# Three edits to a hybrid decoder layer: attention's last score columns, the third channel tile's outputs, and three weight sums

## The chip, the cores and the metric

The kernel runs on one core of one Trainium2 chip. The metric is the device time of one execution, in microseconds (us). Before the change it was 1298.82, 1296.9 and 1293.77 us in three runs, 1296.9 in the median. PE is the matrix engine (TensorE), DVE VectorE, ACT ScalarE, POOL GpSimd, SP SyncE, which issues most of the DMAs.

## What is computed

One decoder layer on 16 meta tokens and 1024 tokens of width 1024, all in float32:

```python
h = jnp.concatenate([meta, x], axis=1)
a = rmsnorm(h, ln_mix_pre[l])
proj = a @ w_in[l]
dq, dk, dv, hq, hf, hi, hg = jnp.split(proj, SPLITS, axis=-1)
y_diff = diff_attention(dq, dk, dv, ...)      # 4 heads, causal, two softmaxes: p[0] - lam * p[1]
y_hgrn = hgrn2(hq, hf, hi, hg, ...)           # 4 heads, a gated recurrence in chunks of 16
mix = jnp.concatenate([y_diff, y_hgrn], axis=-1) @ w_out[l]
h = h + rmsnorm(mix, ln_mix_post[l])
a = rmsnorm(h, ln_ffn_pre[l])
y = conv_ffn(a, w_ffn_up[l], ffn_conv_w[l], ffn_conv_b[l], w_ffn_down[l])
h = h + rmsnorm(y, ln_ffn_post[l])
...
# conv_ffn: u = a @ w_up (5632 channels), a causal convolution of width 3 over the
# sequence for each channel, then gelu(gate) * up, then @ w_down
```

## The kernel before

**Precision.** Every float32 product is made of three matmuls on a high and a low part of each operand (hi x hi, hi x lo, lo x hi). Making the parts is work of ACT (the cast `uh`), and of DVE or POOL (the rest `ul`).

**Order of the work.** The order of PE's rows is written out by the program: generators of attention, recurrence and projections are taken in turn by `interleave`, so that projections fill PE while attention waits. The order on DVE, ACT, POOL and SP is made by the scheduler of the tile layer; `tc.issue_after(x)` pins what is issued within it behind the instruction x. Operations of DVE, ACT and POOL go through one helper and all carry line L58.

**Attention** runs for each of four heads over nine blocks of rows, of which the last, block 8, sees 1040 columns. `scores` (L653 to L707) makes the scores of a block for two maps m, with the projection's rows between them. PSUM is a pool of eight banks (L972): two buffers of one bank under the name `ip`, two of one bank under `m` (`ps_m`, L147), and two of two banks under `S` (`ps_s`, L150). A block up to 912 columns takes one S pair per map. Block 8 takes an S pair for its first 528 columns, and the last 512 stand in E, a tile of its own in an `m` buffer (L691); it is held until the exp of ACT has read it. The `m` buffers serve as well the transposed probabilities `pt` (L722, in `values`, copied out to `at` on ACT or DVE), the weighted values `pa` (L746, in `apply`, fed from `at`) and, from the other helpers, `pn_vh` (L369) and `ssa` (L588). The waits in question stand where block 8's scores are interleaved with `values` and `apply` of block 7.

**The stage between.** The out projection makes y in two halves of 512 columns. For the first half, `out_last` (L1082) adds the last part; `y0_gain` (L1078) multiplies it by the norm's gain on POOL, for blocks from 3 on in the loop at L1302. `post` (L1211) adds the residual (`xh`), norms it and makes the feed-forward input `a`; `trans` (L1242, products at L1250) transposes `a` on PE into `pa`, as the loop goes on with `trans(i - 2)` behind the products of block i. Meanwhile the first weights of the feed-forward part are made ready.

**The feed-forward part** works on 22 tiles of 128 gate channels and 128 up channels each (ft from 0), and on two halves p of the sequence. From tile 1 on a tile is one step of Strassen's method in Winograd's form: seven products j of quarter-size operands, in `unit` (L1395), PE lines L1410 to L1412. Product j of both halves follows one another. The operands are sums of the weight's quarters: `prep` (L1150) loads the four quarters (`ra`, on SP), makes the sums (`ws`, on POOL, in `w_sum`) and splits them (`uh`, `ul`). The loop at L1529 issues the preps of tile ft + 1 in the course of tile ft. DVE adds the products of PSUM to one another: `xu` (product 1 plus product 0), `u`, `uu`, `ug`. The fourth product of a half (j = 3) accumulates in the bank `pb`, which `xu` has to read first.

**Convolution.** When a tile's outputs ug and uu stand, `gated` (L1370) convolves them (per side one operation on ACT, two on DVE, `c`), takes the gelu on ACT, multiplies on POOL and stores to memory (`gsc`). `outputs` (L1356) says where ug and uu stand: for tile 1 in buffers under the name `gk` of the pool `dn` (four buffers a name, otherwise used by the down projection under `gk`, `gh`, `gl` for the gate and its split parts), else in `xup`, which has two buffers a name. Tiles 0 and 1 are not convolved at once: they go on the list `later` (L1437) and are convolved in the tile behind (`ft < 3`, L1536), tile 0 in tile 1 and tile 1 in tile 2. Tile 2 and all further tiles are convolved at once.

The down projection (PE lines L1583 to L1585) follows.

## Time and profile before

| what | us |
|---|---|
| median of three runs | 1296.9 |
| the profiled execution | 1292.96 |
| its span, first to last instruction | 1291.1 |
| PE busy | 1259.6 |
| DVE busy | 887.3 |
| ACT busy | 694.3 |
| POOL busy | 490.8 |

The profile is of one execution. A row of the timeline gives the start in us, the duration, the engine, the line, the operation, out<-in by the program's names without numbers, the shape, how many instructions the row stands for, and in brackets the engine's idle time before it and what ended it. The list of waits sums such idle time by engine, line and releaser. The line of stretches gives for a piece of time the busy time and count of each engine, and the granted clock of PE, where 1.00 is full speed.

### The profile page before, as it was taken

How to read it: one execution, taken by the hardware profiler on the slowest of the kernel's cores; microseconds unless marked ns; L12 is line 12 of the kernel's file. 1: busy time of each engine (PE TensorE's matmuls, PEld its weight loads, DVE VectorE, ACT ScalarE, POOL GpSimd, SP SyncE). 2: the span in 40 equal slices, each digit the busy share in tenths (PEclk: the TensorE clock that was granted, in tenths of full speed). 3: DMA queues.
4: the chain of work that ended last, by engine and by line, in shares of the span. 5: the costliest groups of instructions: out<-in, count | busy, mean ns of one | idle time of the engine just before them, and what ended most of it. 6: DMA issues, size and time to landing. Idle time of an engine off the chain costs nothing.

```text
span 1291.1 us, 26037 instructions
## 1 busy us (share of the span) xinstructions
PE 1259.6 (98%) x10154; PEld 1173.5 (91%) x10154; DVE 887.3 (69%) x1485; ACT 694.3 (54%) x1639; POOL 490.8 (38%) x390
## 2 busy tenths in 40 slices
PE   8999999999999999999998999999999999999996
PEld 7999999999989998777998999999999998878885
DVE  7564646464646563557898778778778786797686
ACT  8465466546654764356764444545445444464543
POOL 5231423141323321353066576676675730010121
PEclk9999999999999999999999999999999999999999
DMA  7335555273734523787312222222222147955363
GB/s 257 95 64 125 88 140 94 77 140 96 131 91 80 123 78 96 224 279 267 132 66 74 75 83 86 78 78 89 80 76 90 66 151 237 339 178 165 89 212 123
DMA packets 116417, 165.04 MB, mean 128 GB/s; under 512 B 10099, under 2 KB 57523, under 8 KB 116294
## 3 DMA queue, kind: packets, MB, share of 16 engines
q1 hardware_dynamic: 93062, 151.84, 36.3%
q0 software_dynamic: 23232, 11.54, 7.6%
q8 instruction: 80, 1.31, 0.4%
q14 instruction: 43, 0.35, 0.1%
HBM read 134.24 MB, written 52.17 MB: 144 GB/s over the span
## 4 chain that ended last, share of the span: by engine, by line
PE 46%; DVE 6%; issue 2%; ACT 1%; DMA 0%; POOL 0%; DVEq 0%; SPq 0%; POOLq 0%; ACTq 0%
PE pd L1584 5%; PE pd L1585 5%; PE pd L1583 5%; PE pb L1410 4%; PE pb L1411 4%; PE pb L1412 4%; PE pc L1411 3%; PE pc L1410 3%; PE pc L1412 3%; PE pa L1411 3%; PE pa L1410 3%; PE pa L1412 3%; DVE c L58 2%; DVE t L58 1%; PE pa L1250 0%
## 5 line engine op out<-in xcount | busy, mean ns | idle before, releaser
L1410 PE MATMUL pb<-t,uh 128*128 128x258 f32 x504 | 141.3, 280 | 4.8 <-DVE xu L58 4.0
L1411 PE MATMUL pb<-t,uh 128*128 128x258 f32 x504 | 141.7, 281 | 0.8 <-DVE t L58 0.8
L1412 PE MATMUL pb<-t,ul 128*128 128x258 f32 x504 | 140.9, 279 | 0.0
L1584 PE MATMUL pd<-wl,gh 128*128 128x512 f32 x308 | 120.3, 391 | 1.1 <-DVE wl L58 1.1
L1585 PE MATMUL pd<-wh,gl 128*128 128x512 f32 x308 | 119.8, 389 | 0.0
L1583 PE MATMUL pd<-wh,gh 128*128 128x512 f32 x308 | 119.8, 389 | 0.0
L58 DVE SCALAR_TENSOR_TENSOR c<-uu,cwt,c 128x514 f32<-128x514 f32 (+1 forms) x88 | 97.1, 1104 | 19.7 <-ACT c L58 19.0
L58 POOL TENSOR_TENSOR c<-c,c 128x514 f32<-128x514 f32 (+1 forms) x44 | 64.7, 1471 | 117.6 <-ACT c L58 115.6
L1410 PEld LDWEIGHTS pb<-t,uh 128*128 128x128 f32 x504 | 95.5, 190 | 5.2 <-DVE xu L58 4.2
L1411 PEld LDWEIGHTS pb<-t,uh 128*128 128x128 f32 x504 | 95.6, 190 | 1.0 <-DVE t L58 1.0
L1412 PEld LDWEIGHTS pb<-t,ul 128*128 128x128 f32 x504 | 95.6, 190 | 0.0
L58 POOL TENSOR_TENSOR ul<-ws,uh 128x512 fp32r<-128x512 f32 x42 | 65.3, 1555 | 78.3 <-ACT uh L58 73.9
L1411 PE MATMUL pa<-t,uh 128*128 128x258 f32 (+1 forms) x336 | 93.9, 279 | 0.0
L1411 PE MATMUL pc<-t,uh 128*128 128x258 f32 (+1 forms) x336 | 93.9, 279 | 0.0
L1410 PE MATMUL pc<-t,uh 128*128 128x258 f32 (+1 forms) x336 | 93.6, 278 | 0.0
L1410 PE MATMUL pa<-t,uh 128*128 128x258 f32 (+1 forms) x336 | 93.6, 278 | 0.0
L1412 PE MATMUL pa<-t,ul 128*128 128x258 f32 (+1 forms) x336 | 93.4, 278 | 0.0
L1412 PE MATMUL pc<-t,ul 128*128 128x258 f32 (+1 forms) x336 | 93.4, 278 | 0.0
L58 DVE SCALAR_TENSOR_TENSOR c<-ug,cwt,c 128x514 f32<-128x514 f32 (+1 forms) x88 | 88.4, 1005 | 0.9 <-ACT c L58 0.3
L58 ACT CAST uh<-ra 128x512 fp32r<-128x512 f32 x67 | 41.4, 619 | 62.1 <-PE pb L1411 37.4
L58 DVE TENSOR_TENSOR ul<-ra,uh 128x512 fp32r<-128x512 f32 x43 | 40.9, 952 | 46.0 <-ACT uh L58 41.0
L1584 PEld LDWEIGHTS pd<-wl,gh 128*128 128x128 f32 x308 | 57.8, 188 | 14.7 <-DVE wl L58 2.8
(389 smaller groups left out, 4166.8 us busy)
## 6 DMA issues: line engine op xcount, KB each, us to landing
ra<-in_wup_dram SPq DMA_DIRECT2D x88, 256.0 KB, 2.7
mp<-msc SPq DMA_DIRECT2D x23, 512.0 KB, 6.0
tsc<-in_wdown_dram SPq DMA_DIRECT2D x44, 256.0 KB, 4.7
wi<-tsc SPq DMA_DIRECT2D x44, 256.0 KB, 3.1
gi<-gsc SPq DMA_DIRECT2D x33, 256.0 KB, 4.5
wi<-in_wdown_dram SPq DMA_DIRECT2D x33, 256.0 KB, 4.8
gsc<-c SPq DMA_DIRECT2D x22, 257.0 KB, 2.0
tsc<-in_wdown_dram POOLq DMA_DIRECT2D x22, 256.0 KB, 7.1
```

The lines of the kernel that those rows point to most:

```text
L58: ins = call(*args, **kw)
L1410: T.matmul(pt, hi[:, s], th[:, k], start=(first and k == 0), stop=False, skip_group_check=True)
L1411: T.matmul(pt, hi[:, s], tl[:, k], start=False, stop=False, skip_group_check=True)
L1412: T.matmul(pt, lo[:, s], th[:, k], start=False, stop=(k == 3), skip_group_check=True)
L1583: T.matmul(py, gh[:, s], wh, start=(k == 0 and pr not in (3, 7)), stop=False, skip_group_check=True)
L1584: T.matmul(py, gh[:, s], wl, start=False, stop=False, skip_group_check=True)
L1585: T.matmul(py, gl[:, s], wh, start=False, stop=(k == NH - 1), skip_group_check=True)
```

## The change

It has three parts; the arithmetic stays the same.

**A.** E takes the first bank of a pair of `S` instead of a buffer of `m`.

**B.** `y0_gain`'s last instruction so far is remembered as `marks["gain"]`, and in tile 1's round of the loop the preps of tile 2 (except product 1's) are issued behind it.

**C.** The outputs of tile 2 stand, like those of tile 1, in the pool `dn`: half p = 0 of both tiles under `gk`, half p = 1 under `gh` and `gl`. Tile 2 goes on the list `later` too, and the loop takes from the list through tile 3. So tile 2 is convolved in tile 3.

```diff
-                        E = ps_m(f"E{nm}_{m}")
+                        E = ps_s(f"E{nm}_{m}")[:, 0]
...
         if i >= 3:
-            y0_gain(i)
+            marks["gain"] = y0_gain(i)
...
     def outputs(ft, p):
-        if ft == 1:
-            return [dn.tile([P, 2 * WN[0]], F32, tag="gk", name=f"{t}{ft}_{p}") for t in ("ug", "uu")]
+        if ft in (1, 2):
+            if p == 0:
+                return [dn.tile([P, 2 * WN[0]], F32, tag="gk", name=f"{t}{ft}_{p}") for t in ("ug", "uu")]
+            return [dn.tile([P, 512], F32R, tag=g, name=f"{t}{ft}_{p}").bitcast(F32) for g, t in (("gh", "ug"), ("gl", "uu"))]
         return [xup.tile([P, 2 * WN[0]], F32, tag=t, name=f"{t}{ft}_{p}") for t in ("ug", "uu")]
...
-        if ft == 1:
+        if ft in (1, 2):
             later.append((ft, p, ug, uu))
...
             if j != 1:
-                prep(7 * (ft + 1) + j)
+                with tc.issue_after(marks["gain"].ins) if ft == 1 else nullcontext():
+                    prep(7 * (ft + 1) + j)
             for u in units:
                 next(u)
-            if ft < 3 and j in (1, 3):
+            if ft < 4 and j in (1, 3):
```

On PE, in head 0, at block 8's scores for the first map (S_8_0 its first 528 columns, E_8_0 the rest); in brackets the engine whose semaphore the row waits for:

```order
 L665 MATMUL S_8_0_1305<-k_0_122,q_0_120 128x264
 L666 MATMUL S_8_0_1305<-kl_112,q_0_120 128x264
-L665 MATMUL E_8_0_1310<-k_0_122,q_0_120 128x512 [waits DVE_49]
+L665 MATMUL E_8_0_1310<-k_0_122,q_0_120 128x512 [waits Activation_49]
 L666 MATMUL E_8_0_1310<-kl_112,q_0_120 128x512
```

No row moved on PE; E_8_0 now waits for ACT, the exp of block 7's second map, whose S pair it takes over. The second map's S_8_1 waits for ACT as well now, and `pt` and `pa` of block 7 wait for other engines than before.

On POOL, in the stage between (y the gains, ws the sums of tile 2's weight quarters, ul a rest of a split):

```order
 L58 TENSOR_TENSOR xh_7053<-xh_7053 2x512
 L58 TENSOR_TENSOR y_6271<-y_6271,gpo_6273 2x512
-L58 TENSOR_TENSOR y_6271<-y_6271,gpo_6273 128x512 x4
+L58 TENSOR_TENSOR y_6271<-y_6271,gpo_6273 128x512 x8
 L58 TENSOR_TENSOR ws_7994<-ra_21_7990,ra_22_7988 128x512
 L58 TENSOR_TENSOR ws_8076<-ws_7994,ra_11_7986 128x512
 L58 TENSOR_TENSOR ws_8112<-ra_11_7986,ra_21_7990 128x512
-L58 TENSOR_TENSOR y_6271<-y_6271,gpo_6273 128x512 x4
 L58 TENSOR_TENSOR ul_7983<-ws_7980,uh_7982 128x512
```

The three sums moved from between the fourth and the fifth gain to behind the eighth. On SP, with them, the load of tile 2's fourth quarter (`ra_12`) moved behind one store of a block, three loads and another store.

On DVE, from the end of tile 2 to product 1 of tile 3 (uu, ug, xu: sums of products of the halves 0 and 1; c_2_0 and c_2_1: the convolution of tile 2 for half 0 and 1), first what stood there before:

```order
 L58 TENSOR_TENSOR uu_0_8264<-pb_0_8299,xu_0_8265 128x258
-L58 SCALAR_TENSOR_TENSOR c_2_0_8503<-uu_0_8264,cwt,c_2_0_8503 128x514
 L58 TENSOR_TENSOR uu_1_8282<-pb_1_8313,xu_1_8283 128x256
-L58 SCALAR_TENSOR_TENSOR c_2_0_8503<-uu_0_8264,cwt,c_2_0_8503 128x514
 L58 TENSOR_TENSOR ug_0_8263<-pc_0_8348,xu_0_8265 128x258
-L58 SCALAR_TENSOR_TENSOR c_2_1_8527<-uu_1_8282,cwt,c_2_1_8527 128x510 x2
-L58 SCALAR_TENSOR_TENSOR c_2_0_8498<-ug_0_8263,cwt,c_2_0_8498 128x514
 L58 TENSOR_TENSOR ug_1_8281<-pc_1_8361,xu_1_8283 128x256
-L58 SCALAR_TENSOR_TENSOR c_2_0_8498<-ug_0_8263,cwt,c_2_0_8498 128x514
-L58 TENSOR_TENSOR ul_8544<-ra_11_8533,uh_8543 128x512
-L58 SCALAR_TENSOR_TENSOR c_2_1_8522<-ug_1_8281,cwt,c_2_1_8522 128x510 x2
-L58 TENSOR_TENSOR xu_0_8549<-pb_0_8583,xu_0_8549 128x258
```

All eight rows of tile 2's convolution stood ahead of tile 3's first `xu`. The rows of the changed program that take their place follow the four sums uu and ug directly:

```order
+L58 TENSOR_TENSOR ul_8522<-ra_11_8511,uh_8521 128x512
+L58 TENSOR_TENSOR xu_0_8527<-pb_0_8561,xu_0_8527 128x258
+L58 TENSOR_TENSOR ul_8603<-ws_8600,uh_8602 128x512
+L58 TENSOR_TENSOR xu_1_8545<-pb_1_8575,xu_1_8545 128x256
+L58 SCALAR_TENSOR_TENSOR c_2_0_8589<-ug_0_8263,cwt,c_2_0_8589 128x514
+L58 SCALAR_TENSOR_TENSOR c_2_0_8594<-uu_0_8264,cwt,c_2_0_8594 128x514
+L58 SCALAR_TENSOR_TENSOR c_2_0_8589<-ug_0_8263,cwt,c_2_0_8589 128x514
+L58 SCALAR_TENSOR_TENSOR c_2_0_8594<-uu_0_8264,cwt,c_2_0_8594 128x514
+L58 TENSOR_TENSOR ul_8639<-ws_8636,uh_8638 128x512
+L58 TENSOR_TENSOR u_3_0_8528<-pb_0_8561,xu_0_8527 128x258
```

The first `xu` of tile 3 now stands ahead of tile 2's convolution; the rows of c_2 stand in tile 3 where those of c_1 stand in tile 2. The rows of c_3, from the end of tile 3 on, keep their places in both programs, ahead of the first `xu` of tile 4, as those of c_2 stood ahead of that of tile 3.

## The prediction

> **What bounds the kernel now.** I read the page first, then what PE waits for, then the rows around each wait. The first two lines of the page give the span and each engine's busy time:

> ```profile
> span 1291.1 us, 26037 instructions
> ...
> PE 1259.6 (98%) x10154; PEld 1173.5 (91%) x10154; DVE 887.3 (69%) x1485; ACT 694.3 (54%) x1639; POOL 490.8 (38%) x390
> ```

> PE is busy for 98% of the span, and the order listing shows the same matmuls in the same order before and after. So the change can win or lose only in PE's idle time, and in PE's clock. These are the waits that the edits bear on (engine, line, engine waited for: us in total, times, longest):

> ```profile
> PE pb L1410 <- DVE xu L58: 4.0, 1, 4.0
> ...
> PE pt L722 <- DVE at L58: 2.3, 4, 1.0
> PE pa L746 <- ACT pb L58: 1.9, 3, 0.8
> PE pa L1250 <- DVE a L58: 1.6, 1, 1.6
> ...
> PE pn_vh L369 <- ACT ona L58: 1.0, 3, 0.3
> ...
> PE pn_vh L369 <- ACT pb L58: 0.6, 1, 0.6
> ```

> The four small ones at L369, L722 and L746 sum to 5.8 us over four heads: the ring of two single-bank buffers in which E stands (edit A). The 1.6 at L1250 stands in the post stage (edit B), the 4.0 at L1410 in channel tile 3 (edit C). What no edit can touch is the other idle time. So the ceiling is 5.8 + 1.6 + 4.0 = 11.4 us, and what a lowered clock costs beside it.

> **A: E out of the two-buffer ring.** Nothing is added; E takes a buffer of the score pairs. The place in head 1 (start, us, engine, what, idle before it), first on PE, then on ACT:

> ```profile
> 229.09 0.39 PE L665 MATMUL E<-k,q 128*128 128x512 f32 x1
> ...
> 231.41 0.55 PE L369 MATMUL pn_vh<-ident,ht 128*128 128x128 f32 x3 [0.32 <-ACT ona L58]
> ...
> 238.56 0.66 PE L722 MATMUL pt<-ident,pb 128*128 128x128 f32 x4 [0.52 <-DVE at L58]
> ...
> 240.66 0.49 PE L746 MATMUL pa<-avn,az 128*128 128x128 f32 x2 [0.83 <-ACT pb L58]
> 240.99 1.73 PE L746 MATMUL pa<-avn,at 128*128 128x128 f32 x14
> ```

> ```profile
> 228.85 0.19 ACT L58 ACTIVATION_READ_ACCUMULATOR pb<-S,ast 128x1 f32 x1
> ...
> 239.84 0.68 ACT L58 ACTIVATE pb<-E,ast 128x512 f32<-128x512 f32 x1
> ...
> 240.50 0.58 ACT L58 COPY at<-pt 128x512 f32<-128x512 f32 x1
> ```

> The three waits sum to 1.67 us here. All three are for buffers that E's long life holds, and all three go. But what is late next is the at copy: pa takes the second four blocks' weights from it. In the rows the second half of pa begins after 8 of the 16 products, at 240.99 + 6 x 1.73 / 15 = 241.7, and the copy ends at 241.08, so it has 0.6 to spare. The copy stands on ACT behind E's exp, which follows E, and E moves up only by the first wait, 0.32. So this head gains 0.32 + 0.6 = 0.9 of its 1.67. By the same limit the four heads together gain their first waits, 1.0 + 0.6 by the two L369 rows, and 0.6 each: 1.6 + 2.4 = 4.0 of the 5.8.

> Against it stands a new wait. E now takes the buffer of S_7_1, and so waits for that block's exp. In the rows the exp's accumulator read ends at 228.85 + 0.19 = 229.04, and E's first product starts at 229.09: just in time. I take a little over 0.1 a head off, so **3.5 us**. Bounds: nothing hides behind at after all and all 5.8 come; or the exp is late by its own read and a little more, and 2 are left.

> **B: the sums pinned behind the last gain.** Three sums of POOL move from before the fifth gain to behind the eighth. PE's two rows at issue, then POOL's, then DVE's:

> ```profile
> 606.13 1.09 PE L1250 MATMUL pa<-ident,a 128*128 128x128 f32 x8 [1.62 <-DVE a L58]
> ...
> 619.65 1.04 PE L1250 MATMUL pa<-ident,a 128*128 128x128 f32 x8
> ```

> ```profile
> 585.06 1.29 POOL L58 TENSOR_TENSOR ws<-ra,ra 128x512 f32<-128x512 f32 x1 [2.46 <-DMA ra<-in_wup_dram]
> 586.42 2.14 POOL L58 TENSOR_TENSOR ws<-ws,ra 128x512 f32<-128x512 f32 x1
> 588.53 1.29 POOL L58 TENSOR_TENSOR ws<-ra,ra 128x512 f32<-128x512 f32 x1
> ...
> 603.71 1.28 POOL L58 TENSOR_TENSOR y<-y,gpo 128x512 f32<-128x512 f32 x1 [3.09 <-ACT jz L58]
> ```

> ```profile
> 588.54 1.82 DVE L58 SCALAR_TENSOR_TENSOR xh<-y,ssy,xh 128x512 f32<-128x512 f32 x1
> 590.29 1.78 DVE L58 SCALAR_TENSOR_TENSOR xh<-tmp,ssy,xh 128x512 f32<-128x512 f32 x1
> ...
> 606.60 0.74 DVE L58 SCALAR_TENSOR_TENSOR xh<-y,ssy,xh 128x512 f32<-128x512 f32 x1
> 607.26 0.74 DVE L58 SCALAR_TENSOR_TENSOR xh<-tmp,ssy,xh 128x512 f32<-128x512 f32 x1
> ...
> 617.71 1.28 DVE L58 SCALAR_TENSOR_TENSOR a<-xh,ssy,gfb 128x1024 f32<-128x1024 f32 x1
> ```

> The same DVE operation lasts 0.74 us with POOL idle and 1.8 while POOL computes. Without the three sums (1.29 + 2.14 + 1.29 = 4.7 us of POOL) the xh pair at 588.54 loses up to 2 x 1.05 = 2.1 us, and the gain behind them starts earlier. The a that PE awaits at 606.13 comes at the end of that chain; I take 1.2 to 2.1 off, so of the 1.62 about 1.3 goes. The sums then run behind the eighth gain, which ended at 603.71 + 1.28 = 605.0, until about 609.7, and there the quick xh pair at 606.60 waits for them instead: up to 2.1 later. The a of two blocks on ends at 617.71 + 1.28 = 618.99, and PE wants it at 619.65, with 0.66 to spare. PE comes 1.3 earlier, and the chain between 607 and 618 has waits of its own that take up part of a delay; I take a delay of 0.4 there, so a new wait of 1.3 + 0.4 - 0.66 = 1.0. Net gain **0.3 us**. Bounds: 1.6 if the delay dies out, and the reverse, -0.5, if it comes through with 1.2. The sums' readers lose nothing, since POOL then stands idle for 48 us (idle before the row), and the load of tile 2's fourth piece, which SP now issues behind the stores and loads of later blocks, is read after that and lands in 2.7 us:

> ```profile
> 653.04 6.70 POOL L58 TENSOR_TENSOR ul<-ws,uh 128x512 fp32r<-128x512 f32 x1 [48.05 <-ACT uh L58]
> ```

> ```profile
> ra<-in_wup_dram SPq DMA_DIRECT2D x88, 256.0 KB, 2.7
> ```

> If that cover were gone, tile 2's first product (672.71, below) would wait for whatever is late beyond it.

> [...]

> **C: tile 2 convolved one tile on.** Before, tile 1's convolution is deferred into tile 2, and tile 2's own follows at once, so that DVE carries two convolutions there and PE starves in tile 3. DVE's three rows, then PE's, then three stretches (length; busy PE, PEld, DVE, ACT, POOL; granted clock; DMA):

> ```profile
> 674.14 0.75 DVE L58 TENSOR_TENSOR uu<-pb,xu 128x258 f32<-128x258 f32 x2
> ...
> 693.48 0.41 DVE L58 TENSOR_TENSOR uu<-pb,xu 128x258 f32<-128x258 f32 x1
> ...
> 704.31 0.41 DVE L58 TENSOR_TENSOR xu<-pb,xu 128x258 f32<-128x258 f32 x1
> ```

> ```profile
> 672.71 0.28 PE L1410 MATMUL pa<-t,uh 128*128 128x258 f32 x1
> ...
> 692.26 0.28 PE L1410 MATMUL pa<-t,uh 128*128 128x258 f32 x1
> ...
> 704.78 0.39 PE L1410 MATMUL pb<-t,uh 128*128 128x258 f32 x1 [3.97 <-DVE xu L58]
> ```

> ```profile
> 606.00:609.00 3.00, 2.87 (x21) 2.47 (x22) 2.00 (x4) 1.03 (x3) 0.00 (x0) 1.00 0.60 191
> ...
> 706.00:709.00 3.00, 3.00 (x16) 3.00 (x16) 1.75 (x3) 0.09 (x1) 3.00 (x3) 0.50 0.23 87
> 709.00:712.00 3.00, 3.00 (x27) 3.00 (x27) 0.85 (x2) 1.00 (x2) 2.92 (x4) 0.97 0.00 0
> ```

> The wait is 3.97 us, and the clock stands at 0.50 behind it: 16 matmuls in 3 us where the next 3 us have 27, so 11 x 0.11 = 1.2 us more. In all 5.2 us hang on this stall.

> The change moves the second load, and takes nothing of it away: tile 3 now carries tile 2's convolution and its own at once. In the order listing, tile 3's rows on DVE, ACT and POOL after stand as tile 2's did before, one tile on. So I shift the measured stretch. From the first uu row of tile 2 to PE's restart there are 704.78 - 674.14 = 30.64 us, in which DVE has almost no idle time. After, the same stretch starts at 693.48 and ends at 724.12. PE wants that product at 704.78 - 3.97 + (692.26 - 672.71) = 720.36. So tile 3's stall goes, and **tile 4's comes, 3.76 us long**, with its clock step: gain 0.2 us. Bounds: 0.5 to lose if the shifted stretch is that much longer (its idle times, near 1 us each, can vary), 5.2 to win if the load, spread otherwise, fits into the tile. The split tiles that now hold tile 2's outputs I cost at nothing: they have four buffers a name, and the store of the gated tile, which SP issues behind three more loads, is read only in the down projection.

> [...]

> **The sum.** 3.5 + 0.3 + 0.2 = 4.0 us. The profiled execution took 1292.96 us (its span 1291.1 and 1.9 around it), so 1289.0 on its scale; it lies 3.9 under the median of 1296.9, to which the same 4.0 gives **1292.9**. That is 0.3%. About 0.5% (6.5 us) is what a measurement of this kernel can tell from no change.

> **The rivals.**

> The stall in tile 4 is shorter or gone. For it: the load that DVE brings into tile 3 may be less than what it brought into tile 2, since POOL and ACT come out of tile 2 with one convolution less, and a stall between 1.62 (no step of the clock) and 3.97 (a step) may or may not bring the step. Against it: the listing, row for row; and POOL and ACT stand at the start of tile 3 as at that of tile 2, 19.3 us on, with the same idle time before them:

> ```profile
> 673.76 1.61 POOL L58 TENSOR_TENSOR c<-c,c 128x510 f32<-128x510 f32 x1 [1.35 <-ACT c L58]
> ...
> 693.09 1.62 POOL L58 TENSOR_TENSOR c<-c,c 128x510 f32<-128x510 f32 x1 [1.34 <-ACT c L58]
> ```

>  Without the clock step 1.2 more goes: 1291.7. Without the stall, 5.2 - 0.2 more: 1287.9.

> A gives nothing, because the change merely turns buffer waits into the wait for S_7_1's exp. For it: 229.04 against 229.09; in each head E would wait about what it spares, and PE, coming earlier, finds the exp not earlier. Against it: the exp stands before the first of the three waits, so only its own lateness costs. Then 1292.9 + 3.5 = 1296.4.

> Slower: the pinned sums hold DVE and POOL for their whole 4.7 us in the chain to the a at 617.71. It then ends at 623.7, and PE, which comes 1.62 earlier, at 618.0, waits 5.7 us and pays the clock step, 1.2. Against the 1.6, 3.5 and 0.2 won that is 1.6 us slower: 1298.5. It decides as soon as a is late by 3.1 us (a wait of 4.1, so that 4.1 + 1.2 makes up for 5.3). [...]

> **How the numbers follow.** Forecast 0.5, with its own range 1290.5 to 1296; the stall gone or the clock spared 0.2 (half each); A without gain 0.2; slower 0.1. The range takes in the rivals but for the ends: 1287.5 to 1298. Faster by over 0.5% (below 1290.4) has most of the stall-gone case and the edge of the forecast with A at its upper bound, 0.26; slower by over 0.5% (above 1303.4) needs the last rival and more beside it, 0.06; within 0.5% is left with 0.68.

> **What would show it.** A: no wait at L369 for ona, L722 for at, or L746 for pb, and a wait of up to 0.7 us within pa for at; wrong, if E at L665 waits for ACT. B: the wait at L1250 near 602 below 0.6 and one of about 1 us some 13 us later; wrong, if the sums still stand before the fifth gain in time, or if the second wait is above 2. C: one wait of 3.5 to 4 us at L1410 for xu some 19.5 us later than now, with the clock at 0.50 behind it; wrong, if no wait above 1 us stands at L1410. The forecast as a whole fails if PE's idle time is not lower by about 4 us.

## The result

The changed kernel takes 1288.54 us in the median of six runs (1287.03 to 1289.11), the kernel before 1293.3 in six (three new ones beside the three known). The ratio is 0.9951, 95% interval 0.9932 to 0.9971: faster by 0.3 to 0.7%, and by 5 to 6 us. The profiled execution took 1287.61 us against 1292.96. A second set of runs of the same kernel (e9_after, below) gave 0.9954 (0.9939 to 0.9969).

The forecast was a gain of 4.0 us and a time of 1292.9, within a range of 1287.5 to 1298, with most of the chance on no change that a measurement could tell. The three mechanisms came as forecast, and the time lies in the range. But the gain came out larger and clear of no change, though 4.0 us stand just at the edge of its interval. And the time had been counted from a median of three runs, 1296.9, where 29 more runs of the same kernel have 1293.72.

### The profile after

The first lines of the page:

```profile
span 1285.5 us, 26038 instructions
...
PE 1258.9 (98%) x10154; PEld 1175.4 (91%) x10154; DVE 887.8 (69%) x1485; ACT 691.9 (54%) x1639; POOL 492.2 (38%) x390
```

PE's work is the same to 0.7 us; the span is 5.6 us shorter. So 4.9 us of the gain are idle time of PE. Its waits after the change (engine, line, releaser: us, times, longest):

```profile
PE pb L1412 <- DVE xu L58: 3.8, 1, 3.8
PE pa L746 <- ACT at L58: 2.9, 4, 1.2
...
PE pa L1250 <- DVE a L58: 0.9, 2, 0.7
```

L1412 is what L1410 was before. Read against the list before: the waits at pn_vh, pt and pa for E's buffers are gone (5.8 us), and one in each head has come, for the at copy (2.9). The wait of 1.6 at L1250 has become two, 0.9 in sum. The wait of 4.0 for xu has become one of 3.8. Now each of the three edits at its place.

**A.** PE in head 1, then ACT:

```profile
227.91 0.50 PE L665 MATMUL E<-k,q 128*128 128x512 f32 x1
...
239.40 0.38 PE L746 MATMUL pa<-avn,at 128*128 128x128 f32 x1 [1.15 <-ACT at L58]
```

```profile
227.67 0.19 ACT L58 ACTIVATION_READ_ACCUMULATOR pb<-S,ast 128x1 f32 x1
...
238.77 0.58 ACT L58 COPY at<-pt 128x512 f32<-128x512 f32 x1
```

The second half of pa starts at 239.40, when the at copy has ended at 239.35: this is what is late next. The prediction expected this wait, of up to 0.7 us a head; in the four heads it is 0.29, 1.15, 1.15 and 0.34. E starts at 227.91, right behind the read at 227.86, and its first product takes 0.50 us instead of 0.39: this is the 0.1 a head that was taken off.

**B.** POOL and DVE where the sums now run, and PE's three products at L1250:

```profile
597.52 1.29 POOL L58 TENSOR_TENSOR y<-y,gpo 128x512 f32<-128x512 f32 x1 [3.08 <-ACT jz L58]
598.77 2.26 POOL L58 TENSOR_TENSOR ws<-ra,ra 128x512 f32<-128x512 f32 x1
601.11 1.62 POOL L58 TENSOR_TENSOR ws<-ws,ra 128x512 f32<-128x512 f32 x1
602.69 1.74 POOL L58 TENSOR_TENSOR ws<-ra,ra 128x512 f32<-128x512 f32 x1
```

```profile
600.41 1.16 DVE L58 SCALAR_TENSOR_TENSOR xh<-y,ssy,xh 128x512 f32<-128x512 f32 x1
601.50 1.77 DVE L58 SCALAR_TENSOR_TENSOR xh<-tmp,ssy,xh 128x512 f32<-128x512 f32 x1
...
612.98 1.28 DVE L58 SCALAR_TENSOR_TENSOR a<-xh,ssy,gfb 128x1024 f32<-128x1024 f32 x1
```

```profile
599.95 1.09 PE L1250 MATMUL pa<-ident,a 128*128 128x128 f32 x8
...
614.32 0.88 PE L1250 MATMUL pa<-ident,a 128*128 128x128 f32 x6 [0.70 <-DVE a L58]
...
624.84 0.55 PE L1250 MATMUL pa<-ident,a 128*128 128x128 f32 x3 [0.21 <-DVE a L58]
```

The first product waits for nothing now. The xh pair beside the sums takes 2.9 us instead of 1.5, the a that PE needs two blocks on ends at 614.26, and PE waits 0.70 for it, and 0.21 once more.

**C.** PE's row of the stall, and the stretches around it (length; busy PE, PEld, DVE, ACT, POOL; granted clock; DMA):

```profile
719.43 0.39 PE L1412 MATMUL pb<-t,uh 128*128 128x258 f32 x1 [3.77 <-DVE xu L58]
```

```profile
716.00:719.00 3.00, 0.00 (x0) 0.00 (x0) 2.96 (x5) 1.63 (x4) 1.55 (x1) 1.00 0.26 90
719.00:722.00 3.00, 2.57 (x15) 2.57 (x16) 2.45 (x6) 1.66 (x3) 2.22 (x2) 0.71 0.24 91
722.00:725.00 3.00, 3.00 (x21) 3.00 (x21) 1.48 (x4) 0.62 (x1) 2.92 (x3) 0.72 0.25 89
725.00:728.00 3.00, 3.00 (x28) 3.00 (x27) 0.56 (x1) 1.27 (x3) 2.91 (x3) 1.00 0.06 20
```

The stall stands one tile on, 3.77 us long against 3.76 forecast, DVE busy through it, and the clock goes down behind it as before (0.71 and 0.72 in two stretches, so half for some 3.4 of the 6 us). That the length agrees to 0.01 us is luck: the prediction allowed 0.5 us for the idle times within the stretch.

### The profile page after: what moved, and what is told of

Same layout as the page of the kernel before. It is cut to its first block, busy times and chain, and to the rows that moved or that the text cites. A ratio compares the mean times of both kernels' runs of the same rounds, so it can differ in the third digit from the quotient of the medians.

```text
span 1285.5 us, 26038 instructions
## 1 busy us (share of the span) xinstructions
PE 1258.9 (98%) x10154; PEld 1175.4 (91%) x10154; DVE 887.8 (69%) x1485; ACT 691.9 (54%) x1639; POOL 492.2 (38%) x390
## 4 chain that ended last, share of the span: by engine, by line
PE 44%; DVE 5%; issue 2%; ACT 2%; POOL 1%; DMA 0%; DVEq 0%; POOLq 0%; ACTq 0%
PE pd L1587 5%; PE pd L1588 5%; PE pd L1586 5%; PE pb L1412 4%; PE pb L1413 4%; PE pb L1414 4%; PE pa L1413 3%; PE pa L1412 3%; PE pa L1414 3%; PE pc L1413 3%; PE pc L1412 3%; PE pc L1414 3%; DVE c L58 2%; DVE xh L58 1%; POOL ws L58 1%
## 5 line engine op out<-in xcount | busy, mean ns | idle before, releaser
L1412 PE MATMUL pb<-t,uh 128*128 128x258 f32 x504 | 141.4, 281 | 4.6 <-DVE xu L58 3.8
L58 DVE SCALAR_TENSOR_TENSOR c<-uu,cwt,c 128x514 f32<-128x514 f32 (+1 forms) x88 | 98.0, 1114 | 18.9 <-ACT c L58 18.3
L58 POOL TENSOR_TENSOR c<-c,c 128x514 f32<-128x514 f32 (+1 forms) x44 | 64.8, 1473 | 113.0 <-ACT c L58 111.0
L1412 PEld LDWEIGHTS pb<-t,uh 128*128 128x128 f32 x504 | 95.6, 190 | 4.9 <-DVE xu L58 4.0
L1412 PE MATMUL pa<-t,uh 128*128 128x258 f32 (+1 forms) x336 | 93.6, 279 | 0.0
L1412 PE MATMUL pc<-t,uh 128*128 128x258 f32 (+1 forms) x336 | 93.6, 278 | 0.0
L58 POOL TENSOR_TENSOR ul<-ws,uh 128x512 fp32r<-128x512 f32 x42 | 65.2, 1552 | 72.5 <-PE pa L1414 43.9
L58 DVE SCALAR_TENSOR_TENSOR c<-ug,cwt,c 128x514 f32<-128x514 f32 (+1 forms) x88 | 89.2, 1013 | 0.9 <-ACT c L58 0.3
L58 ACT CAST uh<-ra 128x512 fp32r<-128x512 f32 x67 | 41.2, 617 | 61.2 <-PE pb L1413 36.2
L58 DVE TENSOR_TENSOR ul<-ra,uh 128x512 fp32r<-128x512 f32 x43 | 40.4, 941 | 46.1 <-ACT uh L58 41.2
## 6 DMA issues: line engine op xcount, KB each, us to landing
ra<-in_wup_dram SPq DMA_DIRECT2D x88, 256.0 KB, 2.7
tsc<-in_wdown_dram SPq DMA_DIRECT2D x44, 256.0 KB, 4.8
wi<-tsc SPq DMA_DIRECT2D x44, 256.0 KB, 3.1
gi<-gsc SPq DMA_DIRECT2D x33, 256.0 KB, 4.1
wi<-in_wdown_dram SPq DMA_DIRECT2D x33, 256.0 KB, 4.6
tsc<-in_wdown_dram POOLq DMA_DIRECT2D x22, 256.0 KB, 7.0
```

The lines of the kernel that those rows point to most:

```text
L58: ins = call(*args, **kw)
L1412: T.matmul(pt, hi[:, s], th[:, k], start=(first and k == 0), stop=False, skip_group_check=True)
```

## The experiments

All times are medians, and all ratios are to the kernel before on the same chip. The runs stand on three chips; differences of up to 1.5 or 2 us between versions of few runs lie within their scatter.

### The three edits, one by one

Each of A, B and C from the change's diff, alone on the kernel before.

A alone. 

> Edit A alone (E in the score pairs), on the kernel before. My theory, from the two traces: A is the bulk of the gain; the waits at pn_vh, pt and pa for E's buffers (5.8 us) go and 2.9 us of waits in pa for ACT's at copy stay, so 2.9 us less idle time at these lines and, with the exp no later, 3 to 4 us in all: about 0.997 of before, 1289.5 us against 1293.3. The stalls at L1250 (1.6) and at xu in tile 3 (4.0) stay as they were. Rival: A's gain is given back further on (the HGRN and out-projection stages wait for the same engines), and the whole gain needs C: then A alone gives under 1.5 us.

Measured: 1289.29 us, ratio 0.9969 (0.9957 to 0.9981). Its waits:

```profile
PE pb L1410 <- DVE xu L58: 4.0, 1, 4.0
PE pa L746 <- ACT at L58: 3.0, 4, 1.2
...
PE pa L1250 <- DVE a L58: 1.9, 2, 1.6
```

The theory holds: about 4 us (2.5 to 5.6), with the other two stalls in their places. Nothing is seen to be given back further on.

B alone. 

> Edit B alone (three sums of tile 2 behind the eighth gain). My theory: the wait of 1.6 us at L1250 goes, and two waits of 0.9 us in sum come 13 and 24 us later, because the sums now run beside the next block's xh pair: net 0.4 us, 0.9997 of before, not to be told from no change by its time. Rival: the first wait's 1.6 us is won in full (then 0.9988) and the later waits came from PE running ahead thanks to A: no wait behind the first in this run.

Measured: 1292.8 us, ratio 0.9988 (0.9977 to 1.0). That is the ratio of the rival, but not by its mechanism: the two later waits are there (0.65 and 0.21 us). The interval reaches from 0 to 3.0 us, so the time alone excludes neither 0.4 nor 1.6.

```profile
PE pa L1250 <- DVE a L58: 0.9, 2, 0.6
```

PE's two rows and DVE's two behind the sums show how the gain goes and comes:

```profile
604.66 1.09 PE L1250 MATMUL pa<-ident,a 128*128 128x128 f32 x8
...
619.02 1.09 PE L1250 MATMUL pa<-ident,a 128*128 128x128 f32 x8 [0.65 <-DVE a L58]
```

```profile
606.21 1.77 DVE L58 SCALAR_TENSOR_TENSOR xh<-tmp,ssy,xh 128x512 f32<-128x512 f32 x1
...
617.68 1.28 DVE L58 SCALAR_TENSOR_TENSOR a<-xh,ssy,gfb 128x1024 f32<-128x1024 f32 x1
```

The first row stands 1.47 us earlier than in the kernel before (606.13), the second 0.63 (619.65). The xh pair began 1.47 earlier and took 1.45 longer, so it ends when it did before (607.98 against 608.00), and so does the a (618.96 against 618.99). From the block ahead of the wait (598.16 against 598.02) to the one behind the second new wait (629.54 against 629.73), PE has won 0.33 us. In the changed kernel it wins 0.35 on the same stretch. So the waits won 0.3 us, less than the list of waits says (1.6 - 0.9 = 0.7), and the rest of the measured 1.5 us is open here.

C alone. 

> Edit C alone (tile 2 convolved in tile 3). My theory: the double load of convolution moves one tile on, with all of its price: the wait of 4.0 us for xu goes from tile 3 and one of 3.8 stands in tile 4, the clock at 0.50 behind it: 0.2 to 0.5 us less than before, 0.9997. Rival: the moved load costs less than the old one (a shorter stall, or a stall without the step of the clock): 1.5 us or more less, and the granted clock behind the stall at 1.00.

Measured: 1294.08 us, ratio 1.0001 (0.999 to 1.0013). C by itself wins nothing that can be measured; the stall stands in tile 4 (3.8 us), and the clock goes down behind it as before. Stretches behind it:

```profile
726.00:729.00 3.00, 2.83 (x18) 2.83 (x19) 2.51 (x6) 1.47 (x3) 2.48 (x2) 0.75 0.35 125
729.00:732.00 3.00, 3.00 (x20) 3.00 (x20) 1.08 (x3) 0.62 (x1) 2.92 (x3) 0.68 0.16 55
```

Added up, the three alone make 0.9969 + 0.9988 + 1.0001 - 2 = 0.9958, beside 0.9951 and 0.9954 for the whole: no interplay beyond the intervals.

### The load is only moved: one tile further

```diff
-        if ft in (1, 2):
+        if ft in (1, 2, 3):
...
-            if ft < 4 and j in (1, 3):
+            if ft < 5 and j in (1, 3):
```

(The first line in `outputs` and where `later` is filled.) 

> All of the change, and C carried one tile further: tiles 1, 2 and 3 are deferred, tile 4 carries its own convolution and that of tile 3. My theory (the load is only moved): the wait of 3.8 us for xu stands in tile 5, some 19.5 us later than in the changed kernel, with the clock step, and the time is that of the changed kernel within 0.3 us (1288.5). Rival (each tile of delay works some of the load off in the idle time of DVE): the stall is shorter than 3 us and the time at least 1 us below the changed kernel's.

Measured: 1288.68 us, ratio 0.9957 (0.9941 to 0.9973), the changed kernel's time. The wait:

```profile
PE pb L1412 <- DVE xu L58: 3.5, 1, 3.5
```

It ends at 739.64, some 20 us behind the changed kernel's, and is 0.2 us shorter. The stall was 3.97, 3.77 and 3.55 us long in tiles 3, 4 and 5: a tile of delay works off some 0.2 us of the load, no more.

### What it takes to be rid of the stall

First, of tile 2 only half p = 1 is deferred, and convolved behind product 1 of tile 3:

```diff
-        if ft in (1, 2):
+        if ft == 1 or (ft, p) == (2, 1):
...
-            if ft < 4 and j in (1, 3):
+            if ft < 3 and j in (1, 3) or (ft, j) == (3, 1):
```

> All of the change, but of tile 2 only half p = 1 is deferred: tile 2 carries three half convolutions, tile 3 three, instead of two and four. My theory (the stall is what a second half load too many adds to DVE's queue, and one is nearly absorbed by DVE's idle time in a tile): the stall of 3.8 us splits into two of 0 to 1 us, no clock step follows, 3.5 to 5 us below the changed kernel: about 1284. Rival (DVE has no room in any tile, every extra operation is paid): two stalls of about 1.9 us each; only the clock step's 1.2 to 1.6 us go: about 1287.

Measured: 1291.08 us, ratio 0.9973 (0.9964 to 0.9983): 2.3 us above the changed kernel on the same chip (1288.75, below). Both theories were wrong. The waits:

```profile
PE pb L1412 <- DVE u L58: 4.3, 2, 3.5
...
PE pb L1412 <- DVE xu L58: 1.1, 2, 0.9
```

The waits for xu did shrink to 1.1, but the deferred half now stands on DVE ahead of tile 3's u sums, behind a first half that had come at once, and PE waits 3.5 for u. The work was split, but put where the next result was due. So the same split with the deferred half behind product 3:

```diff
-            if ft < 3 and j in (1, 3) or (ft, j) == (3, 1):
+            if ft < 3 and j in (1, 3) or (ft, j) == (3, 3):
```

> As the spread of before (of tile 2 only half p = 1 deferred), but that half convolved behind product 3 of tile 3 instead of behind product 1. My theory: the spread lost because the deferred half stood ahead of the u sums of tile 3 on DVE, for which PE then waited 3.5 us; behind them it meets DVE with time to spare. The waits at u fall to the 0.8 that the changed kernel has too, those for xu in tiles 3 and 4 sum to 1 to 2 us, no clock step stands there: 3 to 4.5 us below the changed kernel, about 1285 (0.993). Rival (DVE is full over the two tiles, wherever the work stands): the 3 to 4 us of waiting move on to the xu of tile 4 and the time is that of the changed kernel or above, 1288.5 or more.

Measured: 1287.98 us, ratio 0.9947 (0.9935 to 0.9959), beside 0.9951 and 0.9954 of the changed kernel: not to be told from it, where 3 to 4.5 us were expected. Its waits, and a stretch behind the longest (which ends at 719.23):

```profile
PE pb L1412 <- DVE xu L58: 3.2, 3, 2.1
...
PE pb L1412 <- DVE u L58: 0.8, 1, 0.8
```

```profile
721.00:724.00 3.00, 3.00 (x16) 3.00 (x15) 1.62 (x4) 0.59 (x1) 2.92 (x3) 0.50 0.27 93
```

The place was right: the 3.5 at u is gone. But 0.17, 0.90 and 2.12 us of waits for xu stay, 3.2 where 1 to 2 was expected, and the clock goes down behind 2.12 us too. The truth lies nearer to the rival: by the waits, DVE has room for 0.6 more of the 3.8 us when the work is spread over two tiles, and the time does not show even that.

### What holds A back

Block 7's second at copy on DVE instead of ACT:

```diff
-                (A.copy if pi % 2 else V.tensor_copy)(at[:, lo:n0], pv[:, lo:n0])
+                (A.copy if pi % 2 and i != 7 else V.tensor_copy)(at[:, lo:n0], pv[:, lo:n0])
```

> All of the change, and block 7's second at copy on DVE instead of ACT. My theory (what limits A is that this copy stands on ACT behind E's exp): the four waits in pa for at (2.9 us) go but for 0.5 at most, 2.4 us below the changed kernel: about 1286.1. Rival (the second half of pa is held by something else as well, the az copy or the scores' sums on DVE, which the copy now delays): a wait of another releaser stands there, and under 0.7 us is won.

Measured: 1284.55 us, ratio 0.9927 (0.991 to 0.9944), 4 us below the changed kernel. No wait at L746 is left in the list, and none came in its place in attention. The last of these lines is the largest new one, 1.9 us at L477, ended by nothing that the profile shows; one of 1.8 of that kind, at L1035 in the changed kernel, is gone:

```profile
PE pb L1412 <- DVE xu L58: 3.8, 1, 3.8
PE pg L835 <- DMA grow<-in_gpre_dram: 2.4, 1, 2.4
PE pl L477 <- issue: 1.9, 1, 1.9
```

So the copy behind E's exp is what limited A. It won more than the listed 2.9 us; by the estimate below each of these four waits is short in the list by some 0.17 us, which makes 3.6 of them.

With the first spread (e4_spread) beside it. 

> Both of these additions together on the change. If they are independent, as my theory has it: the sum of what the two runs beside it won, about 1281.5 us. Rival: what PE wins in attention is lost at the next stage that is bound by DVE or ACT, and the sum falls short by more than 1 us.

Measured: 1286.09 us, ratio 0.9943 (0.9925 to 0.9961): the median is 1.5 us above the at copy alone, as the spread alone was 2.3 above the changed kernel. The wait of 3.5 for u is back in the list. So the two add up as far as the scatter of these few runs lets one tell, with the spread's sign turned.

With the second spread (e10_third). 

> The version before this one and the at copy on DVE together. If each saves what it saves alone: 4 below the at copy's 1284.5, about 1281 (0.990). Rival: the two draw on the same DVE time: above 1283.

Measured: 1283.96 us, ratio 0.992 (0.9907 to 0.9933), beside 0.9927 for the at copy alone: not to be told from it. It has the lowest median of all versions, 10 us below the kernel before. The 1281 was missed because the spread had been overrated: the waits for xu are the 3.2 us of the spread alone.

### What B is worth, and the clock

The changed kernel again. 

> The changed kernel itself, unaltered, beside its variants on the same chip: 0.995 to 0.997 of before, a wait of 3.8 us for xu in tile 4, 2.9 us in pa for at. If the first result was helped by its chip or its hour, the ratio is above 0.997.

Measured: 1288.75 us, ratio 0.9954 (0.9939 to 0.9969), with the waits expected.

The sum without B. 

> As the sum, but without edit B, so with the wait of 1.6 us at L1250. Two theories on what B is worth. First (waits alone): 0.35 to 0.7 us, the difference of the waits; then this is under 1 us above the sum, and the clock behind the wait is at 1.00. Second (the wait of 1.6 us lowers the clock in some executions, as it did in the profiles of A alone and of C alone, but not in the first one of before): 1.2 to 2.5 us above the sum, and where the profile has the step, the clock stands at about 0.6 for 3 us behind the wait.

Measured: 1284.89 us, ratio 0.9931 (0.9917 to 0.9944), 0.9 above the sum. It doesn't decide: the wait at L1250 that B is to remove is only 0.39 us in this profile, with 0.46 more 17 us earlier, and the clock there stays at 1.00. The difference of 0.9 is within the scatter besides.

The kernel before, unaltered. 

> The kernel before, unaltered: its time is that of the shared runs (ratio 1.000, within 0.0015). Open is the clock behind its wait of 1.6 us at L1250: at 1.00, as in the first profile, if that wait is too short to lower it and the two steps seen since came from the edits; or at about 0.6, with some 1.6 us more for the same products, if it is chance from execution to execution.

Measured: 1294.07 us, ratio 1.0001 (0.9991 to 1.001). Behind its wait of 1.60 us, which ends at 607.77, the clock is at 1.00:

```profile
607.00:610.00 3.00, 2.23 (x19) 1.96 (x20) 2.65 (x4) 0.99 (x4) 0.00 (x0) 1.00 0.56 160
610.00:613.00 3.00, 3.00 (x15) 2.46 (x14) 1.57 (x2) 2.94 (x11) 0.00 (x0) 1.00 0.99 384
```

In C alone, where the same wait of 1.60 ends at 606.58, it goes down:

```profile
606.00:609.00 3.00, 2.42 (x18) 2.15 (x19) 2.44 (x4) 0.99 (x4) 0.00 (x0) 0.84 0.53 157
609.00:612.00 3.00, 3.00 (x10) 2.33 (x9) 1.78 (x2) 2.94 (x12) 0.00 (x0) 0.60 1.03 390
```

And so it does in A alone, behind the wait of 1.62 that ends at 602.26:

```profile
602.00:605.00 3.00, 2.74 (x19) 2.35 (x20) 2.13 (x4) 1.02 (x2) 0.00 (x0) 0.85 0.58 184
605.00:608.00 3.00, 3.00 (x9) 2.35 (x9) 1.89 (x2) 2.94 (x12) 0.00 (x0) 0.58 0.98 344
```

C alters nothing in this stage. So in four profiles with a wait of 1.6 us here, two of the kernel before and one each of A and C, the clock goes down in two: chance from execution to execution, as far as four show. In the nine profiles with edit B, it stays at 1.00 around L1250.

What a step costs is seen by setting A alone beside the changed kernel, where this stage has no step. Right behind the wait the same product of PE stands at 602.26 and 599.95, 2.31 us apart; when the step is over the same product stands at 607.62 and 603.73, 3.89 apart. So the step costs 1.6 us, and in two executions of four that is 0.8 us on the mean, as an estimate from these four profiles.

The mean granted clock of the runs fits, but decides nothing. Over the 29 runs of before that A, B and C were compared with it is 0.9956, over the 12 of A alone 0.9955, of C alone 0.9951, of B alone 0.9962. A mean higher by 0.0006 is 0.0006 x 1291 = 0.8 us less lost clock; but single runs scatter by 0.001, which makes the difference uncertain by 0.0005 to either side, and the mean also counts the end of the program (in the profile of before, 5 us at 0.50 in which PE has no product left). The changed kernel's two sets of runs have 0.9957 and 0.9958.

## Why the prediction missed

**The sum, by its terms.** A 3.5, B 0.3, C 0.2, together 4.0; measured alone 0.9969, 0.9988 and 1.0001, which on 1293.7 is 4.0, 1.5 and -0.1, together 5.4 (the whole: 6.3 and 6.0 by its two ratios, 4.8 and 5.1 by medians).

**A: right, a little small.** What is late next was named rightly, and the cap of 4.0 by it is the time measured for A alone. What was taken off for E's wait was too much, if anything. But the lists seem to say less, 5.8 before and 2.9 after. Two neighbouring rows of before show why:

```profile
239.54 0.29 PE L250 MATMUL pi_hg<-alo,wh_hg 128*128 128x272 f32 x1
240.66 0.49 PE L746 MATMUL pa<-avn,az 128*128 128x128 f32 x2 [0.83 <-ACT pb L58]
```

From issue to issue 1.12 us pass, where the same product is followed by the next after 0.12 elsewhere: PE stood for 1.0, and 0.83 is listed: the list counts from the end of the row ahead, 239.54 + 0.29 = 239.83, and the next product would have started at 239.66. So this wait is short in the list by 0.17 us. If all of this kind are, as an estimate from this one, eleven waits have become four, 7 x 0.17 = 1.2, and 2.9 + 1.2 = 4.1. The prediction had worked with starts of rows and so come to 4.0.

**B: the step that failed.** The price of the waits came out: net 0.3 was forecast, and in starts of rows PE wins 0.33. By its parts that is partly luck, for of the 1.62 all goes instead of 1.3, the a is not delayed at all instead of by 0.4, and PE waits twice behind it instead of once. What failed is that the wait at L1250 was priced by its length alone, because the one profile of before showed the clock at 1.00 behind it. In two of four profiles it isn't: then 3.4 us run at half speed (604.11 to 607.52 in A alone, at 0.50), which costs 1.6. That chance was B's to remove, and it was put at nothing. With 0.8 for it B comes to 1.1, beside 1.5 measured (0 to 3.0). So the step is shown and its price is read from rows; that it is what B alone won on the mean is an estimate, since the interval of that run is too wide to tell.

With A at 4.1, B at 1.1 and C at 0.2 the three make 5.4 us, where 4.0 was forecast and 4.8 to 6.3 was measured.

**C: right.** The stall moved, 3.77 us long against 3.76, at the tile and the row named, and with its clock step. The edit alone is worth nothing that a run can tell (1.0001); 0.2 was forecast. The rival, a shorter stall, was wrong.

**The clock.** The prediction took 1.62 us as a wait without a step of the clock and 3.97 us as one with it, each from the one profile of before, and kept the step for the stall of 3.76. The clock did go down behind 3.77 us (0.71 and 0.72 in two stretches of 3 us). But it fell behind 1.60 us (0.84 and 0.60, C alone), 1.62 (0.85 and 0.58, A alone) and 2.12 us (0.50, second spread) as well, so here a wait of 1.6 us is not safe.

**The slower rival** had the sums hold the a at 617.71 for 4.7 us. In B alone they held its chain for 1.45 us, the time by which the xh pair got longer, and the chain had started 1.47 earlier, so the a came when it had come before.

**The time and the chances.** Of the 4.4 us between 1292.9 and 1288.54, 3.6 are the base: the median of three runs, 1296.9, was taken as the kernel's time, though the profiled execution at 1292.96 stood below all three, and six runs have 1293.3. 1289.0, the figure on the profile's scale, was within 0.5 of the result. And "about 0.5% is what a measurement can tell" was too coarse: the intervals are 0.1 to 0.2% to either side, so a forecast of 0.3% should not have been called no change. The gain by ratio, 0.49%, lies at the very edge between the prediction's case of no change (chance 0.68) and its case of faster by over 0.5% (0.26).

## What to carry to other kernels

When a wait for a buffer goes, look for what the same instruction needs next, in starts of rows: that gives the gain. The list of waits only points to it: A won 4.1 us where 5.8 were listed, and moving the at copy won about 4 where 2.9 were. Work that overfills an engine isn't made much less by deferring all of it a stage (the stall was 3.97, 3.77 and 3.55 us in tiles 3, 4 and 5); a split helps only where the pieces stand behind the results that are due next. Here that place was worth some 3 us (0.9973 against 0.9947), and the split itself nothing that the time shows. Here a wait of the matrix engine cost its length and, behind two of four waits of 1.6 us, a lowered clock (1.6 us more in A alone), so one profile without the step is not enough to leave it out, and the base of a forecast is better taken from the profiled execution and the runs together than from the median of three.

## What was not expected of the hardware

The scatter of this kernel's runs goes with the clock: among the 29 runs of before, the five with a mean granted clock of 0.997 took 1291.49 to 1294.32 us, and the four at 0.993 and 0.994 1295.39 to 1299.76. The steps named here come behind waits of 1.04 to 3.97 us, at places that vary: the second profile of before had one at 515 us, behind a wait of 1.04 us for ACT, which the first had not.

```profile
600.70:604.11 3.41, 1.85 (x17) 1.67 (x18) 3.41 (x4) 1.46 (x6) 0.43 (x1) 1.00 0.61 178
604.11:607.52 3.41, 3.41 (x9) 2.63 (x9) 1.63 (x3) 3.29 (x11) 0.00 (x0) 0.50 0.99 369
```

```profile
604.10:607.51 3.41, 2.08 (x10) 1.38 (x8) 1.73 (x1) 3.38 (x13) 1.28 (x1) 1.00 0.91 293
607.51:610.92 3.41, 3.15 (x23) 2.70 (x24) 2.13 (x4) 1.40 (x4) 0.00 (x0) 1.00 0.63 198
```

In A alone the wait of 1.62 us lies almost whole in one piece, PE is busy for 1.85 of its 3.41 us, and the clock goes down to 0.50. In the other profile the piece ends at 607.51, 0.26 us before the wait of 1.60 does, PE is busy for 2.08, and the clock stays at 1.00. In the second spread the wait of 2.1 us for xu lies almost whole in one piece (717.28 to 720.69, PE busy for 1.47), and the step follows. With the at copy moved as well, it ends at 715.81 and lies in two pieces (counted back from the half-clock stretch at the program's end, at 1275.04), the first has 1.86 us of PE, and no step follows. But in the first profile of before the piece from 603.34 to 606.75 holds the whole wait and 1.79 us of PE, and the clock stays at 1.00 all the same. So these numbers don't tell the waits with a step from those without: of those that lie whole or almost whole in one piece, 1.85 and 1.47 us of PE were followed by it and 1.79 was not. What decides it is not shown here.
